# Up projection: eight products with high weight parts, then eight with low parts, where one of each took turns

## The chip, the core and the metric

The kernel runs on one core of a Trainium2 chip. The metric is device time in microseconds for one execution, as the median of several. Everything is float32 at the interface.

The engines that matter here are TensorE (matrix products; its weight loads are shown on a row of their own, PEld), VectorE (DVE), ScalarE (ACT), GpSimd (POOL) and SyncE (SP), which issues the transfers from memory.

## What is computed

One layer of a decoder trunk on 256 positions and 2048 channels. The sub-layer that the change touches, cut from the reference:

```python
h = rms_norm(x, norm2_g[l]) * (1.0 + scale2) + shift2
up = causal_dwconv(h @ w_up[l], ffn_dw_w[l], ffn_dw_b[l])    # w_up: 2048 x 11264
val, gt = jnp.split(up, 2, axis=-1)
x = x + gate2 * ((jax.nn.silu(gt) * val) @ w_down[l])        # w_down: 5632 x 2048
```

Before it stands a mixer sub-layer (an input projection, a causal convolution of width 31, a position mixing, an output projection), and shift, scale and gate come from a product of a conditioning vector with 2048 x 12288 weights.

## The kernel before

**Two-part operands.** TensorE multiplies operands in a reduced float32 form (float32r in the code). To keep float32 accuracy, an operand is split: `hi` is its rounded copy (ScalarE, line 154), `lo` is what is left (VectorE, line 155). A full product is then hi x hi + hi x lo + lo x hi.

**Weight tiles.** `load_split` brings in one tile of weights, 128 partitions x 2048 float32 (1 MB), into `raw` (4 buffers), and splits it into `hi` and `lo` (3 buffers each). It returns two halves of 1024 columns. Each half holds eight blocks of 128 x 128, for eight steps of the contraction.

**The up projection.** Its 11264 output columns are 88 blocks of 128: 44 value blocks and 44 gate blocks. The contraction over 2048 channels has `KT` = 16 steps of 128. The normalised activations are kept as a pair: `h2_of(k)` holds, for step k, 256 high values and behind them 256 low values per partition, 512 in one stretch. One product with the high part of the weights (`mm_up`, line 680) streams all 512 and writes 512 columns of an accumulator, which covers hi x hi and hi x lo. One product with the low part (line 681) streams the 256 high values alone and adds to the first 256 columns, which covers lo x hi. The accumulator is one bank of 128 x 512 float32. A block of weights is the operand that is loaded into the array; the activations are streamed.

`up_first` makes the first two column pairs, four accumulators at once, while the activations are still being made. `up(p)` makes each other pair of a value and a gate block, p = 2 to 43: for each of the two, one weight tile, 16 steps, and in each step a 512-wide product and a 256-wide one in turn. `up_f` then adds the two halves of the accumulators, applies the width-3 convolution, silu and the product, and splits the result for the down projection (lines 687 to 705, on ScalarE and VectorE).

**Order.** Each engine takes its instructions in program order, except where a few are given higher priority. `pump` puts pieces of background work (the modulation products of line 199, on VectorE with their own 1 MB transfers) behind each pair, by a credit in microseconds. The sequence is: `up_first`, `up` for pairs 2 to 23, the down projection of these (`down`, lines 183 to 185, products of 512 columns), `up` for pairs 24 to 43, the down projection of the rest.

Names in the profile: `pup` is the accumulator of the up projection, `hi_up`, `lo_up` and `raw_up` its weights, `h2a_h2b` its activations, `pod` the accumulator of the down projection, `pg`, `pu`, `pvc`, `pa`, `pco` those of stages in the mixer whose products are 256 wide, and `powo` that of the mixer's output projection (512 wide).

Of the kernel before, what the change touches and what calls it, by code (L numbers as in the profile page):

```python
# [17 lines left out]
P = 128  # L18
D = 2048
S = 256  # L20
NT = S // P
KT = D // P
# [44 lines left out]
def trunk(ctx, tc, xin, cvec, rows, wada, wa0, wa1, wv, wu, wg, wso, wco, wsT, wout, wup0, wup, wdn, out):  # L67
    nc = tc.nc
# [7 lines left out]
    def psum(name="ps"):  # L76
        return pp.tile([P, 512], F32, tag="ps", name=name)
# [86 lines left out]
    def load_split(src, name, places=None):  # L164

        raw = load_raw(src, name)
        if places is None:
            hi = wp.tile([P, 2048], F32R, tag="hi", name=f"hi_{name}", bufs=HI_BUFS)
            lo = wp.tile([P, 2048], F32R, tag="lo", name=f"lo_{name}", bufs=HI_BUFS)
        else:  # L170
            hi, lo = places[:, 0, :], places[:, 1, :]
        last["split"] = split(hi, lo, raw)
        return [(hi[:, h * 1024:(h + 1) * 1024], lo[:, h * 1024:(h + 1) * 1024]) for h in range(2)]
# [76 lines left out]
    def gate_half(j, kh):  # L250
        ps = psum(f"pg{kh}{j}")
        parts = load_split(wg[kh, j], f"g{kh}{j}")
        for half in range(2):
            hi, lo = parts[half]
            for kk in range(8):
                k = 8 * kh + kk
                cs = slice(kk * P, (kk + 1) * P)
                mm3(ps[:, half * S:(half + 1) * S], hi[:, cs], lo[:, cs], hH[:, k, :], hL[:, k, :], kk == 0, kk == 7)
        return ps

    for k in range(KT):
# [9 lines left out]
        hi = wp.tile([P, 2048], F32R, tag="hi", name=f"hi_a{k}", bufs=HI_BUFS)[:, :n0]  # L271
        lo = wp.tile([P, 2048], F32R, tag="lo", name=f"lo_a{k}", bufs=HI_BUFS)[:, :n0]
        split(hi, lo, raw)
        for j in range(4 + NV // 2):
            for half in range(2):
                cs = slice((2 * j + half) * P, (2 * j + half + 1) * P)
                mm3(pa[j][:, half * S:(half + 1) * S], hi[:, cs], lo[:, cs], hH[:, k, :], hL[:, k, :],
                    k == 0 and half == 0, k == KT - 1, skip_group_check=True)
        if k >= 8:
            for j in (2 * (k - 8), 2 * (k - 8) + 1):  # L280
                ps = gate_half(j, 0)
# [6 lines left out]
    def pump(phase, pe, dve):  # L288

        fill, share = SHARES[phase]  # L290
        us = fill * pe - dve
        if not (bg["conv"] and bg["ada"]):
            share = 1.0 if bg["conv"] else 0.0
        for key, part in (("conv", us * share), ("ada", us * (1 - share))):
            credit[key] += part
            while bg[key] and credit[key] >= bg[key][0][0]:
                cost, f = bg[key].pop(0)
                credit[key] -= cost
                f()
            if not bg[key]:  # L300
                credit[key] = 0.0
# [132 lines left out]
    for j in range(8):  # L434
        if j < NV:
            ps = pa[4 + j // 2][:, (j % 2) * S:(j % 2 + 1) * S]
        else:
            ps = psum(f"pvc{j}")[:, :S]
# [54 lines left out]
    for j in range(4, 8):  # L493
        ps = psum(f"pa{j}")
# [18 lines left out]
    for j in range(8):  # L513
        ps = psum(f"pu{j}")
# [7 lines left out]
    for j in range(KT):  # L522
        ps = gate_half(j, 1)
# [7 lines left out]
    for j2 in range(8):  # L531
        raw = load_raw(wso[j2], f"so{j2}")
        ps = psum(f"pso{j2}")
# [17 lines left out]
    for j2 in range(8):  # L551
        parts = load_split(wco[j2], f"co{j2}")
        ps = psum(f"pco{j2}")
# [104 lines left out]
    def h2_of(k):  # L658
        return h2[k // 8][:, k % 8, :, :]
# [14 lines left out]
    fslots = (2, 4, 5, 6, 0, 1)  # L674
    fH, fL = {}, {}

    def mm_up(ps, hi, lo, k):

        hk = h2_of(k)
        nc.tensor.matmul(ps, hi, hk.rearrange("p a s -> p (a s)"), start=(k == 0), stop=(k == KT - 1), skip_group_check=True)  # L680
        nc.tensor.matmul(ps[:, :S], lo, hk[:, 0, :], start=False, stop=(k == KT - 1), skip_group_check=True)  # L681

    def up_sum(dst, ps, jj):

# [8 lines left out]
    def up_f(p, ps):  # L693
        yv = t2(f"yv{p}").rearrange("p (h s) -> p h s", h=2)
        for half in range(2):
            up_sum(yv[:, half, :], ps[half], p + half * NF)
        sl = t1(f"sl{p}")
        nc.scalar.activation(sl, yv[:, 1, :], AF.Silu)
        f = t1(f"f{p}")
        nc.vector.tensor_tensor(f, yv[:, 0, :], sl, op=ALU.mult)  # L700
        if p % 4 == 0:
            ft = slot(fslots[(p // 4) % 6], [P, 4, 2, S], f"f{p}", F32R)
            for q in range(4):
                fH[p + q], fL[p + q] = ft[:, q, 0, :], ft[:, q, 1, :]
        split(fH[p], fL[p], f)

    def up(p):
        ps = [psum(f"pup{p}{half}") for half in range(2)]
        for half in range(2):
            parts = load_split(wup[2 * (p - 2) + half], f"up{p}{half}")  # L710
            for k in range(KT):
                hi, lo = parts[k // 8]
                cs = slice((k % 8) * P, (k % 8 + 1) * P)
                mm_up(ps[half], hi[:, cs], lo[:, cs], k)
        up_f(p, ps)
        pump("up", 10.3, 7.6)

    def up_first():

        ps = [psum(f"pup0{i}") for i in range(4)]  # L720
        for k4 in range(4):
            with ExitStack() as behind:
                if k4 >= 1:
                    behind.enter_context(tc.issue_after(last["dve"].ins))
                if k4 >= 2:
                    behind.enter_context(tc.issue_after(last["act"].ins))
                parts = load_split(wup0[k4], f"up0{k4}") if k4 else up0[0]
            for kk in range(4):
                k = 4 * k4 + kk
                i = make_h2(k)  # L730
                if k <= AFTER_K:
                    last["dve"] = i
                hi, lo = parts[kk // 2]
                for i in range(4):
                    cs = slice(((kk % 2) * 4 + i) * P, ((kk % 2) * 4 + i + 1) * P)
                    mm_up(ps[i], hi[:, cs], lo[:, cs], k)
        for p in range(2):
            up_f(p, ps[2 * p:2 * p + 2])
# [5 lines left out]
    for p in range(2, SEG):  # L744
        up(p)
# [4 lines left out]
    for p in range(SEG, NF):  # L750
        up(p)
# [79 lines left out]
```

## Time and profile before

| | |
|---|---|
| median of 3 runs | 1377.37 us (1373.61 to 1377.42) |
| profiled execution, its own time | 1376.01 us |
| its span, first to last instruction | 1374.3 us |
| mean granted TensorE clock | 0.986 |
| TensorE busy | 1327.7 us, 97% of the span |
| VectorE busy | 1073.5 us, 78% |
| ScalarE busy | 649.8 us, 47% |
| up projection, pairs 2 to 23 | about 654 to 899 us of the span |
| up projection, pairs 24 to 43 | about 1032 to 1255 us |

Times in the views count from the first instruction. A matmul's recorded duration runs from its start to its modelled end, and the next one starts before that end, so the distance between starts, not the duration, tells how fast TensorE takes them. In a row such as "128x512 f32", the number behind the x is how many columns a product streams.

### The profile page before, as it was taken

What the parts mean: (1) busy time and instruction counts of PE and PEld (TensorE: products, weight loads), DVE (VectorE), ACT (ScalarE), POOL (GpSimd) and SP (SyncE); (2) the same over time, 40 slices, a digit from 0 to 9 for tenths busy, and PEclk for the clock granted to TensorE, in tenths of its full rate; (3) what the DMA queues carried; (4) which work ended last, traced back from release to release, by engine and by line L of the source; (5) the groups of instructions that cost most, each with busy time, mean ns of one, the idle gap of its engine ahead of it and who ended that gap; (6) DMA issues with size and microseconds to landing.
All of it is one profiled execution on the core that took longest, in us unless ns stands there. A gap on an engine that the chain in (4) does not pass through costs nothing.

```text
span 1374.3 us, 19691 instructions
## 1 busy us (share of the span) xinstructions
PE 1327.7 (97%) x8170; PEld 1195.6 (87%) x8170; DVE 1073.5 (78%) x1319; ACT 649.8 (47%) x772; POOL 6.9 (1%) x18
## 2 busy tenths in 40 slices
PE   5689999999999999998999999999999999999997
PEld 4689999999999899887888888888888888888885
DVE  6987789999999698888998887754456776776573
ACT  5244464545551344445555555543334555555351
POOL 0000000000000000000000000000000000000000
PEclk9899999999999999998999999999999999999999
DMA  9999887687776898895877775555555555554551
GB/s 349 371 360 336 339 314 274 225 297 273 291 292 260 304 361 338 322 336 196 316 295 284 285 286 184 184 184 187 200 194 184 186 192 194 194 185 184 191 206 62
DMA packets 49481, 350.89 MB, mean 255 GB/s; under 512 B 5488, under 2 KB 5488, under 8 KB 8432
## 3 DMA queue, kind: packets, MB, share of 16 engines
q1 hardware_dynamic: 49392, 349.63, 68.6%
q8 instruction: 64, 1.05, 0.3%
q14 instruction: 25, 0.20, 0.0%
HBM read 347.51 MB, written 2.10 MB: 254 GB/s over the span
## 4 chain that ended last, share of the span: by engine, by line
PE 93%; DVE 3%; DMA 3%; ACT 1%; issue 0%; POOL 0%; ACTq 0%; POOLq 0%; SPq 0%
PE pup L680 24%; PE pup L681 12%; PE pod L184 6%; PE pod L183 6%; PE pod L185 6%; PE pg L179 4%; PE pg L177 4%; PE pg L178 4%; PE pso L537 4%; PE powo L184 2%; PE powo L185 2%; PE powo L183 2%; DVE ada L199 2%; PE pa L179 2%; PE pa L177 2%; PE pa L178 2%
## 5 line engine op out<-in xcount | busy, mean ns | idle before, releaser
L680 PE MATMUL pup<-h2a_h2b,hi_up 128*128 128x512 f32 x1408 | 494.1, 395 | 0.9 <-DVE h2a_h2b L237 0.9
L681 PE MATMUL pup<-h2a_h2b,lo_up 128*128 128x256 f32 x1408 | 395.7, 281 | 0.0
L680 PEld LDWEIGHTS pup<-h2a_h2b,hi_up 128*128 128x128 f32 x1408 | 266.3, 189 | 62.7 <-DVE h2a_h2b L237 1.3
L155 DVE TENSOR_TENSOR lo_up<-raw_up,hi_up 128x2048 fp32r<-128x2048 f32 x88 | 201.6, 2291 | 82.7 <-ACT hi_up L154 82.7
L681 PEld LDWEIGHTS pup<-h2a_h2b,lo_up 128*128 128x128 f32 x1408 | 265.0, 188 | 0.0
L199 DVE SCALAR_TENSOR_TENSOR ada<-ada,cbc 128x2048 f32<-128x2048 f32 x96 | 219.4, 2291 | 15.3 <-ACT cbc L129 7.7
L154 ACT ACTIVATE hi_up<-raw_up 128x2048 fp32r<-128x2048 f32 x88 | 168.6, 1916 | 110.0 <-PE pup L680 83.7
L155 DVE TENSOR_TENSOR lo_d<-raw_d,hi_d 128x2048 fp32r<-128x2048 f32 x42 | 96.3, 2292 | 92.2 <-ACT hi_d L154 92.2
L179 PE MATMUL pg<-hH_hL,lo_g 128*128 128x256 f32 x512 | 143.2, 280 | 0.4 <-DVE lo_g L155 0.4
L177 PE MATMUL pg<-hH_hL,hi_g 128*128 128x256 f32 x512 | 143.1, 279 | 0.0
L178 PE MATMUL pg<-hH_hL,hi_g 128*128 128x256 f32 x512 | 142.8, 279 | 0.0
L154 ACT ACTIVATE hi_d<-raw_d 128x2048 fp32r<-128x2048 f32 x42 | 80.5, 1916 | 107.1 <-PE pod L185 106.1
L184 PE MATMUL pod<-lo_d,f 128*128 128x512 f32 x332 | 129.2, 389 | 0.0
L183 PE MATMUL pod<-hi_d,f 128*128 128x512 f32 x332 | 129.2, 389 | 0.0
L185 PE MATMUL pod<-hi_d,f 128*128 128x512 f32 x332 | 129.2, 389 | 0.0
L179 PEld LDWEIGHTS pg<-hH_hL,lo_g 128*128 128x128 f32 x512 | 96.2, 188 | 0.6 <-DVE lo_g L155 0.6
L178 PEld LDWEIGHTS pg<-hH_hL,hi_g 128*128 128x128 f32 x512 | 96.0, 187 | 0.0
L177 PEld LDWEIGHTS pg<-hH_hL,hi_g 128*128 128x128 f32 x512 | 95.9, 187 | 0.0
L177 PE MATMUL pa<-hH_hL,hi_a 128*128 128x256 f32 x256 | 72.1, 300 | 19.6 <-ACT hH_hL L236 19.6
L155 DVE TENSOR_TENSOR lo_g<-raw_g,hi_g 128x2048 fp32r<-128x2048 f32 x32 | 74.5, 2328 | 18.5 <-ACT hi_g L154 18.5
L324 DVE SCALAR_TENSOR_TENSOR yc<-apad,cv,yc 128x256 f32<-128x256 f32 x200 | 85.7, 495 | 0.2
L689 ACT ACTIVATE yv<-pl,cv 128x256 f32<-128x256 f32 x88 | 50.9, 596 | 63.8 <-DVE pl L688 63.8
(196 smaller groups left out, 2299.5 us busy)
## 6 DMA issues: line engine op xcount, KB each, us to landing
ada<-in SPq DMA_DIRECT2D x96, 1024.0 KB, 5.8
raw_up<-in SPq DMA_DIRECT2D x88, 1024.0 KB, 4.8
raw_d<-in SPq DMA_DIRECT2D x44, 1024.0 KB, 4.8
raw_g<-in SPq DMA_DIRECT2D x32, 1024.0 KB, 6.2
raw_wo<-in SPq DMA_DIRECT2D x16, 1024.0 KB, 4.9
raw_a<-in SPq DMA_DIRECT2D x16, 640.0 KB, 5.6
raw_a<-in SPq DMA_DIRECT2D x8, 1024.0 KB, 4.8
raw_u<-in SPq DMA_DIRECT2D x8, 1024.0 KB, 4.9
```

What stands on the lines that cost most here:

```text
L154: nc.scalar.activation(hi, src, AF.Copy)
L155: return nc.vector.tensor_tensor(lo, src, hi.bitcast(F32), op=ALU.subtract)
L177: nc.tensor.matmul(ps, wH, aH, start=start, stop=False, **kw)
L178: nc.tensor.matmul(ps, wH, aL, start=False, stop=False, **kw)
L179: nc.tensor.matmul(ps, wL, aH, start=False, stop=stop, **kw)
L183: nc.tensor.matmul(ps, aH, wH, start=start, stop=False, **kw)
L184: nc.tensor.matmul(ps, aH, wL, start=False, stop=False, **kw)
L185: nc.tensor.matmul(ps, aL, wH, start=False, stop=stop, **kw)
L199: nc.vector.scalar_tensor_tensor(w, w, 1.0, cbc, op0=ALU.mult, op1=ALU.mult, accum_out=dst)
L324: nc.vector.scalar_tensor_tensor(ycf[:, j, :], src, cv[:, w0 + k:w0 + k + 1], ycf[:, j, :], op0=ALU.mult, op1=ALU.add)
L680: nc.tensor.matmul(ps, hi, hk.rearrange("p a s -> p (a s)"), start=(k == 0), stop=(k == KT - 1), skip_group_check=True)
L681: nc.tensor.matmul(ps[:, :S], lo, hk[:, 0, :], start=False, stop=(k == KT - 1), skip_group_check=True)
```

## The change

In `up`, the order of the 32 products of each weight tile is changed; `mm_up` is cut into two functions for it. Each half tile's eight products with the high part come first, for steps 0 to 7, then the eight with the low part, for the same steps. Then the second half follows likewise. The products themselves, their operands, the accumulators and the flags are the same. `up_first` keeps one of each in turn.

```diff
-    def mm_up(ps, hi, lo, k):
+    def mm_up_hi(ps, hi, k):
 
-        hk = h2_of(k)
-        nc.tensor.matmul(ps, hi, hk.rearrange("p a s -> p (a s)"), start=(k == 0), stop=(k == KT - 1), skip_group_check=True)
-        nc.tensor.matmul(ps[:, :S], lo, hk[:, 0, :], start=False, stop=(k == KT - 1), skip_group_check=True)
+        nc.tensor.matmul(ps, hi, h2_of(k).rearrange("p a s -> p (a s)"), start=(k == 0), stop=(k == KT - 1), skip_group_check=True)
+
+    def mm_up_lo(ps, lo, k):
+        nc.tensor.matmul(ps[:, :S], lo, h2_of(k)[:, 0, :], start=False, stop=(k == KT - 1), skip_group_check=True)
+
+    def mm_up(ps, hi, lo, k):
+        mm_up_hi(ps, hi, k)
+        mm_up_lo(ps, lo, k)
...
             parts = load_split(wup[2 * (p - 2) + half], f"up{p}{half}")
-            for k in range(KT):
-                hi, lo = parts[k // 8]
-                cs = slice((k % 8) * P, (k % 8 + 1) * P)
-                mm_up(ps[half], hi[:, cs], lo[:, cs], k)
+
+            for kh in range(2):
+                hi, lo = parts[kh]
+                for part, mm in ((hi, mm_up_hi), (lo, mm_up_lo)):
+                    for kk in range(8):
+                        mm(ps[half], part[:, kk * P:(kk + 1) * P], 8 * kh + kk)
```

## The prediction

> **What bounds the kernel now.** I read the page first: its span, the busy shares, the chain that ended last and the costliest groups. The chain's first line gives engines, its second names lines. In a group, the number before the bar is the count, then come busy time, mean ns of one, and idle time before the group with what ended it.
>
> ```profile
> span 1374.3 us, 19691 instructions
> ...
> PE 1327.7 (97%) x8170; PEld 1195.6 (87%) x8170; DVE 1073.5 (78%) x1319; ACT 649.8 (47%) x772; POOL 6.9 (1%) x18
> ...
> PE 93%; DVE 3%; DMA 3%; ACT 1%; issue 0%; POOL 0%; ACTq 0%; POOLq 0%; SPq 0%
> PE pup L680 24%; PE pup L681 12%; PE pod L184 6%; PE pod L183 6%; PE pod L185 6%; PE pg L179 4%; PE pg L177 4%; PE pg L178 4%; PE pso L537 4%; PE powo L184 2%; PE powo L185 2%; PE powo L183 2%; DVE ada L199 2%; PE pa L179 2%; PE pa L177 2%; PE pa L178 2%
> ...
> L680 PE MATMUL pup<-h2a_h2b,hi_up 128*128 128x512 f32 x1408 | 494.1, 395 | 0.9 <-DVE h2a_h2b L237 0.9
> L681 PE MATMUL pup<-h2a_h2b,lo_up 128*128 128x256 f32 x1408 | 395.7, 281 | 0.0
> ```
>
> TensorE is the bound: 93% of the chain, and 36% of it in the two lines that the change reorders. In all 2816 of their products it sat idle 0.9 us, once, at the very start. So there is no wait here to remove. Only the rate at which TensorE takes the products can change, and each ns per product goes straight to the end.
>
> The mean ns of a matmul overlaps its neighbours and is no rate. The rate comes from first and last start. The instructions by tile give these in a stretch (columns: count, duration min/median/max in ns, first to last start); for the accumulator of the up projection from 660 to 880 us:
>
> ```profile
> L680 PE MATMUL pup<-h2a_h2b,hi_up x632: 392/392/396, 659.8 to 879.9; 128*128 128x512 f32 x158
> L681 PE MATMUL pup<-h2a_h2b,lo_up x631: 278/280/283, 660.0 to 879.8; 128*128 128x256 f32 x158
> ```
>
> (879.9 - 659.8) us over 631 steps is 348.8 ns for a pair of one 512-wide and one 256-wide product. Half a weight tile is eight pairs, 2790 ns. The change makes that eight wide products and then eight narrow ones.
>
> **What runs of one width cost.** The same view for stages where one width repeats, the first two in threes (three lines take turns):
>
> ```profile
> L183 PE MATMUL pod<-hi_d,f x163: 389/389/389, 909.7 to 1019.9; 128*128 128x512 f32 x163
> ...
> L178 PE MATMUL pg<-hH_hL,hi_g x228: 279/279/279, 334.8 to 415.0; 128*128 128x256 f32 x114
> ...
> L177 PE MATMUL pco<-aH,hi_co x111: 283/283/283, 489.7 to 529.3; 128*128 128x256 f32 x111
> ```
>
> Wide in a run: 110.2 us / (162 x 3) = 226.7 ns. Narrow in a run: 80.2 us / (227 x 3) = 117.8 ns in the gates, 39.6 us / (110 x 3) = 120.0 ns in the conv output. The timeline (start, duration) holds a third steady rate for narrow ones, in a V tile:
>
> ```profile
> 206.17 0.28 PE L178 MATMUL pvc<-hH_hL,hi_v 128*128 128x256 f32 x1
> ...
> 211.27 0.28 PE L178 MATMUL pvc<-hH_hL,hi_v 128*128 128x256 f32 x1
> ```
>
> Fifteen rounds of three in 5.10 us is 113.3 ns, with moving data from the same pair of tiles as the gates. So the narrow rate has states, and I cannot tell from here which one a run of eight will fall into.
>
> 226.7 + 117.8 = 344.5 ns against 348.8 measured: taking turns costs 4.3 ns per pair more than the two widths cost in runs of their own. That is the whole prize. Pairs that the change touches: 42 column pairs x 2 halves = 84 weight tiles x 16 = 1344, in 168 half tiles (the other 64 of 1408, in the first two column pairs, keep their order).
>
> **The change, part by part.**
>
> *Wide run and narrow run.* 8 x (226.7 + 117.8) = 2756 ns against 2790: 34 ns less per half tile. Bounds for the narrow one: 113.3 and 120.0. For the wide one the lower end is 226.7; the upper comes from the border between up and down projection, where wide products start right behind a narrow one:
>
> ```profile
> 1255.32 0.28 PE L681 MATMUL pup<-h2a_h2b,lo_up 128*128 128x256 f32 x1
> 1255.44 0.39 PE L183 MATMUL pod<-hi_d,f 128*128 128x512 f32 x1
> 1255.67 0.39 PE L184 MATMUL pod<-lo_d,f 128*128 128x512 f32 x1
> ...
> 1257.28 0.39 PE L185 MATMUL pod<-hi_d,f 128*128 128x512 f32 x1
> ...
> 1031.92 0.39 PE L185 MATMUL pod<-hi_d,f 128*128 128x512 f32 x1
> 1032.14 0.40 PE L680 MATMUL pup<-h2a_h2b,hi_up 128*128 128x512 f32 x1
> 1032.38 0.28 PE L681 MATMUL pup<-h2a_h2b,lo_up 128*128 128x256 f32 x1
> ```
>
> The first eight steps there take 1.84 us, 230 ns each, before 226.7 is reached. I take the settled 226.7 and 117.8, since most rows of hundreds of products stand at them, and keep 230 and 120.0 as the dear end, 226.7 and 113.3 as the cheap one.
>
> *The switches.* Sixteen alternations become one switch each way. The first wide step after a narrow one was 0.23 us, about 3 ns over 226.7. The last wide step before a narrow one was 0.24 at 1032.14, but alternation was starting there; I take 3 ns for it too. Toll: 6 ns per half tile; between 0 and some 16 (13 at one by 1032.14, 3 at the other).
>
> *Waits for the split.* The first narrow product of a weight tile, which waits for VectorE's low part, moves back by seven wide products, 7 x 0.227 = 1.6 us. That gains nothing, as TensorE's waits in the whole program show (waiter, releaser: us, times, longest):
>
> ```profile
> PE pa L177 <- ACT hH_hL L236: 19.6, 9, 3.4
> ...
> PE pup L680 <- DVE h2a_h2b L237: 0.9, 1, 0.9
> ```
>
> No row names the up projection's weights. If VectorE fell behind, the new order would hide up to 1.6 us of it per tile; nothing is late, so I book zero.
>
> *Release of the high buffer.* The last wide product of a tile is now followed by eight narrow ones (8 x 0.118 = 0.94 us), where one followed (0.12 us). ScalarE's copy for the tile three on waits for just that release, and VectorE's subtraction for the copy:
>
> ```profile
> ACT hi_up L154 <- PE pup L680: 83.7, 54, 3.6
> ...
> DVE lo_up L155 <- ACT hi_up L154: 82.7, 64, 3.2
> ```
>
> Both, the release of the raw buffer and the next transfer in SyncE's queue behind it start up to 0.8 us earlier. Neither engine is late, so zero; what would be late next is VectorE, while the background modulation work runs:
>
> ```profile
> 654.00:700.00 46.00, 46.00 (x265) 40.28 (x265) 41.94 (x55) 25.98 (x36) 0.00 (x0) 1.00 0.82 310
> ```
>
> These are, for 654 to 700 us, length, busy time of TensorE, its loads, VectorE (41.94 of 46 us, 91%), ScalarE and GpSimd, the granted clock and DMA share. A tile shorter by 0.06 of 5.58 us asks 92% of VectorE: still covered. No instruction, byte or semaphore is added; start and stop flags fall on the same products.
>
> **The sum.** 34 - 6 = 28 ns x 168 = 4.7 us. The profiled execution took 1376.0 us, 1.7 over its span; it would take 1371.3, the span 1369.6. The median of the runs is 1377.37, so I forecast 1372.7 us. All of it must appear inside the two stretches of up projection.
>
> A rule that speaks against the change stands in the Trainium skill, "TensorE: Matmul & The Clock Gate", section Back-to-back issue gap: a warm product holds TensorE for its width at 2.4 GHz plus 2.5 ns. By it a pair is an estimated 215.8 + 109.2 = 325 ns in any order and the time would stay 1377.4. The trace has 226.7, 117.8 and 348.8 in those places, so a surplus that the rule lacks is there, and whether it follows order is the question; the section LDWEIGHTS of that page (128 columns, an estimated 107 ns) gives no preference either, since eight loads lie under narrow products in both orders.
>
> **The rivals.**
>
> *The settled rate is not reached* (24%). Eight wide products are just the unsettled stretch of 1255.44: 8 x (230 + 117.8) = 2782, 8 ns less, x 168 = 1.4 us: 1376.0. For: that border shows wide products straight behind a narrow one with no pause between, as each half tile now will, and they took seven steps to settle. Against: the down projection streams the weights and holds the activations, the other way round from here, so its settling need not carry over.
>
> *The surplus belongs to place, not order* (14%). The 4.3 ns could come from where the second normalised activations lie against the weights, for no other stage streams from them: no change, 1377.4. For: narrow rates of 117.8 and 120.0 differ with the stage. Against: 113.3 and 117.8 occur on the same tiles, so phase matters also without a move.
>
> *Cheap narrow state* (10%): 8 x (226.7 + 113.3) = 2720, 70 - 6 = 64 ns x 168 = 10.8 us: 1366.6.
>
> *Dear state* (4%): 8 x (230 + 120) = 2800, +10 ns x 168 = 1.6 us: 1379.0.
>
> *Slower: each switch restarts the load pipeline* (5%). Where a stage begins, the second product is late, as if its weights had not been fetched ahead:
>
> ```profile
> 285.47 0.36 PE L177 MATMUL pu<-hH_hL,hi_u 128*128 128x256 f32 x1
> 285.67 0.28 PE L178 MATMUL pu<-hH_hL,hi_u 128*128 128x256 f32 x1
> 285.79 0.28 PE L179 MATMUL pu<-hH_hL,lo_u 128*128 128x256 f32 x1
> ```
>
> 0.20 in place of 0.12. If both switches paid 0.085 us: 170 - 34 = 136 ns x 168 = 22.8 us, 1400.2. It makes the kernel slower by 0.3% from (34 + 25) / 2 = 30 ns per switch on. Against: width changed at every product so far without it, and at 1255.44 and 1032.14 the toll was 3 and 13 ns.
>
> **How the numbers follow.** The settled case holds the remaining 43%. Below, 0.3% (4.1 us) is about what a measurement can tell from no change. The settled case with a toll of 0 to 16 ns gives 5.7 to 3.0 us, so some three quarters of it, and the cheap state, count as faster: 0.32 + 0.10, and a little for a partly cheap narrow run in the unsettled case, 0.46. Slower: the restart and a share of the dear state, 0.07. The rest, 0.47, is the same. The range runs from the cheap state, 1366.5, to the dear one, 1379.0, and leaves out the restart and what lies beyond the bounds; the likeliest case alone spans 1371.7 to 1374.4.
>
> **What would show it.** Right: eight starts of the high line some 227 ns apart, then eight of the low line some 118 apart, 2.76 us per half tile, and the same stretches elsewhere to the ns. Starts of 230 throughout the high run show the second case; 113 in the low run the cheap one; a single step of 0.30 or 0.20 at a switch, the restart. The wait of ScalarE's copy for TensorE should shrink or move by about 0.8 us per tile without any end moving. The prediction is wrong if the wide rate on these activations has a floor above 227, if the narrow runs take 120, or if a wait for a low part appears on TensorE.

## The result, and the profile after

The changed kernel takes 1368.68 us (median of 8 runs, 1364.01 to 1370.60) against 1377.39 us for the kernel before (8 runs, 1372.58 to 1379.96). The ratio is 0.994, 95% interval 0.9925 to 0.9955: faster by 0.45 to 0.75%. A second comparison on another occasion, told below, gave 0.992, interval 0.9903 to 0.9938. The profiled execution took 1364.01 us, its span 1362.3.

From the page after: span, busy time by engine, the chain, and the groups of the up projection's products (now lines 679 and 682).

```profile
span 1362.3 us, 19690 instructions
...
PE 1318.1 (97%) x8170; PEld 1188.4 (87%) x8170; DVE 1072.2 (79%) x1319; ACT 649.3 (48%) x772; POOL 6.9 (1%) x18
...
PE 93%; DVE 4%; DMA 2%; ACT 1%; issue 0%; POOL 0%; ACTq 0%; POOLq 0%; SPq 0%
...
L679 PE MATMUL pup<-h2a_h2b,hi_up 128*128 128x512 f32 x1408 | 359.0, 392 | 0.9 <-DVE h2a_h2b L237 0.9
...
L682 PE MATMUL pup<-h2a_h2b,lo_up 128*128 128x256 f32 x1408 | 201.4, 279 | 0.0
```

TensorE is as much the bound as before and waits as little. The two groups' busy times are a trap: they add up to 560 us where they were 890, for a saving of some 6 us. Busy time is the union of overlapping spans, and turn-taking made the two lines overlap each other. The share of TensorE, 97% before and after, shows nothing of the change either. The Trainium skill warns that matmul busy time is no good measure of how close a kernel is to its roofline, the most that the engine could do ("Perfetto Trace Analysis", section Identifying the Most-Contended Engine). These traces agree: 97% in both, at two different rates.

What shows it is the distance between starts. The timeline after merges the runs of eight (start, time, line, count):

```profile
664.47 2.00 PE L679 MATMUL pup<-h2a_h2b,hi_up 128*128 128x512 f32 x8
666.30 1.07 PE L682 MATMUL pup<-h2a_h2b,lo_up 128*128 128x256 f32 x8
667.21 1.99 PE L679 MATMUL pup<-h2a_h2b,hi_up 128*128 128x512 f32 x8
669.03 1.11 PE L682 MATMUL pup<-h2a_h2b,lo_up 128*128 128x256 f32 x8
669.98 2.00 PE L679 MATMUL pup<-h2a_h2b,hi_up 128*128 128x512 f32 x8
```

Eight wide products take 1.83 and 1.82 us, 228 to 229 ns each; eight narrow ones take 0.91 us (113.8 each) in the first half of a tile and 0.95 (118 to 119) in the second. A tile is 669.98 - 664.47 = 5.51 us, where it was 16 x 348.8 ns = 5.58.

Where the profiled spans differ by 12.0 us, the first and last starts of the low-part products, and of the high-part ones, locate it. Before, then after:

```profile
L680 PE MATMUL pup<-h2a_h2b,hi_up x1408: 392/392/793, 628.9 to 1255.1; 128*128 128x512 f32 x176
...
L681 PE MATMUL pup<-h2a_h2b,lo_up x1408: 278/280/415, 629.5 to 1255.3; 128*128 128x256 f32 x176
```

```profile
L679 PE MATMUL pup<-h2a_h2b,hi_up x1408: 388/392/796, 623.8 to 1242.3; 128*128 128x512 f32 x176
...
L682 PE MATMUL pup<-h2a_h2b,lo_up x1408: 276/279/415, 624.4 to 1243.4; 128*128 128x256 f32 x176
```

The up projection began 5.1 us earlier; from its first to its last product it took 619.6 us in place of 626.4, 6.8 less; what follows took 119.0 and 118.9. Of the 6.8, about 5.8 are 84 tiles at 0.069 us. Some 1.2 lie in the first pairs, whose order did not change: up to the first read of an accumulator they took 24.5 us at a granted clock of 0.87 before, and 23.3 at 0.93 after (length, busy times, then the clock in the column after GpSimd's):

```profile
628.90:653.40 24.50, 24.45 (x124) 21.29 (x125) 21.86 (x33) 12.28 (x19) 0.00 (x0) 0.87 0.44 146
```

```profile
623.80:647.10 23.30, 23.29 (x124) 20.29 (x125) 22.04 (x33) 12.25 (x19) 0.00 (x0) 0.93 0.45 159
```

So the change accounts for 5.8 us between these two executions; the mixer's 5.1 and the first pairs' 1.2 needed an explanation, or to be shown as chance. For the first pairs, later profiles of the same two kernels gave 24.1 us at a clock of 0.90 and 23.7 at 0.91: their length went with the granted clock, and it moved by 0.4 us between executions of one kernel.

### The profile page after: what moved, and what is told of

Read it like the earlier page. It is cut to its first block, busy times and chain, and to the rows that moved or that the text cites. A ratio compares the mean times of both kernels' runs of the same rounds, so it can differ in the third digit from the quotient of the medians.

```text
span 1362.3 us, 19690 instructions
## 1 busy us (share of the span) xinstructions
PE 1318.1 (97%) x8170; PEld 1188.4 (87%) x8170; DVE 1072.2 (79%) x1319; ACT 649.3 (48%) x772; POOL 6.9 (1%) x18
## 4 chain that ended last, share of the span: by engine, by line
PE 93%; DVE 4%; DMA 2%; ACT 1%; issue 0%; POOL 0%; ACTq 0%; POOLq 0%; SPq 0%
PE pup L679 24%; PE pup L682 12%; PE pod L185 6%; PE pod L184 6%; PE pod L183 6%; PE pg L179 4%; PE pg L177 4%; PE pg L178 4%; PE pso L537 4%; PE powo L185 2%; PE powo L183 2%; PE powo L184 2%; DVE ada L199 2%; PE pa L179 2%; PE pa L177 2%; PE pa L178 2%
## 5 line engine op out<-in xcount | busy, mean ns | idle before, releaser
L679 PE MATMUL pup<-h2a_h2b,hi_up 128*128 128x512 f32 x1408 | 359.0, 392 | 0.9 <-DVE h2a_h2b L237 0.9
L679 PEld LDWEIGHTS pup<-h2a_h2b,hi_up 128*128 128x128 f32 x1408 | 253.0, 188 | 45.9 <-DVE h2a_h2b L237 1.3
L154 ACT ACTIVATE hi_up<-raw_up 128x2048 fp32r<-128x2048 f32 x88 | 168.6, 1916 | 96.5 <-PE pup L679 72.8
L682 PEld LDWEIGHTS pup<-h2a_h2b,lo_up 128*128 128x128 f32 x1408 | 192.4, 188 | 13.9
L682 PE MATMUL pup<-h2a_h2b,lo_up 128*128 128x256 f32 x1408 | 201.4, 279 | 0.0
L179 PEld LDWEIGHTS pg<-hH_hL,lo_g 128*128 128x128 f32 x512 | 96.2, 188 | 1.2 <-DVE lo_g L155 1.2
```

Source lines behind the costliest of these rows:

```text
L154: nc.scalar.activation(hi, src, AF.Copy)
L179: nc.tensor.matmul(ps, wL, aH, start=False, stop=stop, **kw)
L679: nc.tensor.matmul(ps, hi, h2_of(k).rearrange("p a s -> p (a s)"), start=(k == 0), stop=(k == KT - 1), skip_group_check=True)
L682: nc.tensor.matmul(ps[:, :S], lo, h2_of(k)[:, 0, :], start=False, stop=(k == KT - 1), skip_group_check=True)
```

## The experiments

A weight tile's time below is read from the instructions by tile, in a window that holds 40 whole tiles of the first stretch and the first product of the next: count 641, and (last - first start) / 40.

### The kernel before, once more

No edit.

> The kernel before once more, unchanged, for its spread. Theory A (only the rate at which TensorE takes the up projection's products changed): a weight tile of the up projection takes 5.58 us again, to the ns, while the start of the up projection (628.9 us before, 623.8 us after the change) moves by several us from one execution to another of the same kernel. Rival (the change also moves the mixer): the start stays within 1 us of 628.9.

It took 1378.02 us, span 1376.3. High-part products in the first stretch (40 tiles) and in the second (38 tiles):

```profile
L680 PE MATMUL pup<-h2a_h2b,hi_up x641: 392/397/398, 658.7 to 884.8; 128*128 128x512 f32 x161
...
L680 PE MATMUL pup<-h2a_h2b,hi_up x609: 392/392/396, 1039.7 to 1251.9; 128*128 128x512 f32 x153
...
L680 PE MATMUL pup<-h2a_h2b,hi_up x1408: 392/396/792, 628.1 to 1257.1; 128*128 128x512 f32 x176
```

226.1 us / 40 = 5.65 us a tile in the first stretch, 212.2 / 38 = 5.58 in the second. Theory A missed this: turn-taking has two rates, 353.3 and 348.8 ns a pair, and the same program falls into one or the other. The profile on which I predicted had the cheap one in both stretches. A dear first stretch costs 44 x 0.07 = 3.1 us more. In the timeline the dear pattern repeats after three pairs: 231, 117, 234, 123, 237, 118 ns between starts; the cheap one has 229 to 232 and 117 to 120. The start of the up projection, 628.1, lies within 1 us of 628.9, as the rival has it; that it moves without the change had yet to be seen.

### Runs of two and of sixteen

```diff
-            for kh in range(2):
-                hi, lo = parts[kh]
-                for part, mm in ((hi, mm_up_hi), (lo, mm_up_lo)):
-                    for kk in range(8):
+            for k0 in range(0, KT, 2):          # or 16
+                for which, mm in ((0, mm_up_hi), (1, mm_up_lo)):
+                    for k in range(k0, k0 + 2):
...
```

> Two products with high parts, then two with low parts, instead of eight and eight. Theory A1 (each switch of width costs something, about 34 ns saved per 8 pairs over 7 switches saved each way): half of the switches are gone, so about half of the gain, 5.55 us a weight tile. Theory A2 (no price per switch; the products fall into a repeating pattern whose phase the run length sets): anything between 5.49 and 5.60 us, not in proportion. Rival B (the earlier release of the high buffer brings the gain): the release comes 0.12 us earlier only, so 5.57 to 5.58 us.

> All sixteen products with high parts of a weight tile, then all sixteen with low parts. A1: half of the remaining switches gone, 5.508 us a tile or a little less than 5.513; if the wide ones settle at 226.7 ns after eight steps, 16 x 226.7 + 16 x 115 is about 5.48 us. A2: not in proportion, 5.49 to 5.60. B: released 0.94 us earlier again, so more of the gain, under 5.513 us.

1369.39 and 1369.62 us (one run each; the kernel before beside them 1378.21). In runs of two, then of sixteen:

```profile
L679 PE MATMUL pup<-h2a_h2b,hi_up x641: 388/392/394, 658.3 to 879.1; 128*128 128x512 f32 x161
```

```profile
L679 PE MATMUL pup<-h2a_h2b,hi_up x641: 388/392/397, 658.8 to 879.5; 128*128 128x512 f32 x161
```

5.520 us and 5.518, against 5.513 with eight. A price per switch (A1) falls: with four times the switches, runs of two lose 0.007 of the 0.069 us, where half was expected; halving the switches gains nothing. The release (B) does not fit either: runs of two release the buffer hardly earlier, and have nearly the whole gain. What costs is taking turns at every single product. That fits A2, a repeating pattern, though the spread that A2 allowed was wide.

### High parts last in the second half tile

```diff
-                for part, mm in ((hi, mm_up_hi), (lo, mm_up_lo)):
+                two = ((hi, mm_up_hi), (lo, mm_up_lo))
+                for part, mm in two if kh == 0 else two[::-1]:
```

> First half tile as in the changed kernel, second half with the low products first: runs of 8, 16 and 16, and the last high product ends the tile, so the high buffer is released later than even before the change. A: the rate of runs, 5.48 to 5.52 us a tile. B (release): no gain, 5.58 us or more, and a wait for the split on TensorE.

1369.93 us. The buffer's release is now the last thing that a tile does, and nothing is lost (its high-part products, then the row of TensorE's waits that names the up projection):

```profile
L679 PE MATMUL pup<-h2a_h2b,hi_up x641: 388/392/397, 658.8 to 879.5; 128*128 128x512 f32 x161
```

```profile
PE pup L679 <- DVE h2a_h2b L237: 1.3, 1, 1.3
```

220.7 / 40 = 5.518 us, and TensorE's only wait in the up projection is still the one at its start. The release (B) is no part of the gain.

### The accumulators apart

```diff
+        lows = [psum(f"plow{p}{half}")[:, :S] for half in range(2)]
...
-        nc.tensor.matmul(ps[:, :S], lo, hk[:, 0, :], start=False, ...)
+        nc.tensor.matmul(low, lo, hk[:, 0, :], start=(k == 0), ...)
...
         nc.vector.tensor_tensor(pl, pl, ps[:, :S], op=ALU.add)
+        nc.vector.tensor_tensor(pl, pl, low, op=ALU.add)
```

> The kernel before, one of each in turn, but in pairs 2 to 43 the low-part products add up in a bank of their own, so that consecutive products never write the same accumulator; VectorE adds the second bank with one more 256-wide instruction per block (some 0.42 us, 84 of them). Stream theory (the surplus of turn-taking lies in how streamed data and weight loads of changing length fall against each other): a weight tile takes 5.58 or 5.65 us as with one bank. Accumulator theory (it lies in two widths that write one bank in turn): the surplus goes, 5.51 us or less.

1376.97 us (the kernel before beside it 1375.80). The first three tiles, then 35 tiles from the ninth on, and four rows of the timeline between:

```profile
L680 PE MATMUL pup<-h2a_h2b,hi_up x49: 392/397/398, 654.3 to 671.3; 128*128 128x512 f32 x49
...
L680 PE MATMUL pup<-h2a_h2b,hi_up x561: 392/392/396, 699.6 to 895.0; 128*128 128x512 f32 x187
```

```profile
676.80 0.28 PE L684 MATMUL plow<-h2a_h2b,lo_up 128*128 128x256 f32 x1
677.07 0.70 PE L680 MATMUL pup<-h2a_h2b,hi_up 128*128 128x512 f32 x2
...
688.44 0.63 PE L680 MATMUL pup<-h2a_h2b,hi_up 128*128 128x512 f32 x2
688.91 0.40 PE L684 MATMUL plow<-h2a_h2b,lo_up 128*128 128x256 f32 x2
```

17.0 / 3 = 5.67 us and 195.4 / 35 = 5.58: the same two rates, so two widths in one bank are not the cause. The run also shows a change of pattern. It starts in the dear one. At 676.8 the steps are disturbed (0.27 us where 0.12 is usual, then two wide products in a row and two narrow ones), and by 678.5 the dear pattern is back. At 688.44 two wide and two narrow products come in a row again, this time without a pause, and behind them the cheap pattern stays for good. So the pattern hangs on how the sequence was entered.

### The streamed data moved

The pair of activations has some room in its buffer; `H_AT` places the mixer's pair, `H2_AT` the up projection's, in bytes.

```diff
-H_AT, H2_AT = 64, 320
+H_AT, H2_AT = 0, 0          # runs of eight; then 320, 64
+H_AT, H2_AT = 192, 0        # one of each in turn; then 448, 64
+H_AT, H2_AT = 192, 192      # runs of eight
```

> The changed kernel with the second pair of activations 320 bytes further down in its buffer (offset 0 in place of 320), as the conv output's activations lie; the first pair, which the mixer streams, at 0 in place of 64. Place theory (the surplus over the width hangs on where the streamed data lie against the weights): wide products settle at 226.7 ns and narrow ones at 120.0, as in the stages that lie so: 16 x 346.7 = 5.55 us a weight tile; the gates go from 117.8 to 120.0. Phase theory (the products fall into one of a few repeating patterns that order and start choose, wherever the data lie): 5.51 us a tile as before the move, the gates stay at 113.3 or 117.8.

> The changed kernel with the second pair at 64 in place of 320, where the mixer's pair lies, and the first pair at 320. Place theory: another rate than 5.513 us a tile, and the gates leave 117.8 for the rates seen in the up projection's narrow runs. Phase theory: 5.51 us, the gates at 113.3 or 117.8.

> The kernel before (one of each width in turn) with the second pair at 0 in place of 320, the first at 192. Place theory: the 348.8 and 353.3 ns a pair seen in two executions of the kernel before both go, to one new value, 346.7 by the stages that lie at 0. Phase theory: one of the two, 5.58 or 5.65 us a tile, or a third, not under 5.55, and it may change at the down projection between the two stretches.

> The kernel before with the second pair at 64, the first at 448. Place theory: a value of its own, different from that at 0. Phase theory: as at 0, 5.58 or 5.65 us a tile.

> The changed kernel with both pairs of activations at 192 in their buffer (64 and 320 before). With the first pair at 192 or 448 the gates ran at 113.3 ns a narrow product for long stretches. If the place decides which pattern the products fall into, the up projection's narrow runs all take 113.3 ns in place of 113.3 and 118 by halves: 5.513 - 8 x 0.0045 = 5.48 us a tile, and the gates start at 113.3. If the phase at the start of a stretch decides, 5.51 us, and the gates show either rate.

Single runs: 1382.80, 1368.05, 1376.43, 1372.55 (the kernel before beside these four 1374.95), and 1367.01 us (1375.80). In that order, high-part products of 40 tiles (behind the first a row of its gates, behind the fourth its second stretch):

```profile
L679 PE MATMUL pup<-h2a_h2b,hi_up x641: 389/393/398, 666.2 to 889.7; 128*128 128x512 f32 x161
...
L177 PE MATMUL pg<-hH_hL,hi_g x223: 283/283/283, 339.7 to 419.7; 128*128 128x256 f32 x112
```

```profile
L679 PE MATMUL pup<-h2a_h2b,hi_up x641: 388/392/394, 657.5 to 878.0; 128*128 128x512 f32 x161
```

```profile
L680 PE MATMUL pup<-h2a_h2b,hi_up x641: 395/398/403, 654.3 to 880.4; 128*128 128x512 f32 x161
```

```profile
L680 PE MATMUL pup<-h2a_h2b,hi_up x641: 392/397/398, 653.3 to 879.4; 128*128 128x512 f32 x161
...
L680 PE MATMUL pup<-h2a_h2b,hi_up x609: 392/392/396, 1034.3 to 1246.4; 128*128 128x512 f32 x153
```

```profile
L679 PE MATMUL pup<-h2a_h2b,hi_up x641: 388/393/398, 653.7 to 875.6; 128*128 128x512 f32 x161
```

| place of the up projection's pair | runs of eight | one of each in turn |
|---|---|---|
| 0 | 5.588 us | 5.653 in both stretches |
| 64 | 5.513 | 5.653, then 5.582 in the second stretch |
| 192 | 5.548 | not tried |
| 320 (as it was) | 5.513 | 5.582 or 5.653 |

Each pure theory was half right, and neither gave the tile times at 0 and 192 with runs (5.55 and 5.48 by place, 5.51 by phase). Place sets the rates: with runs of eight at 0, narrow products take 120.0 ns but the first, and every wide run starts with unsettled steps of 228 to 236, like those at the border in the prediction; the gates went from 117.8 to 80.0 us / (222 x 3) = 120.1 ns. But 64 and 320 give the same rates, and at either, turn-taking has the same two. Runs beat turn-taking at 0 too, by some 0.065 us a tile. That the run at 0 took 1382.80 us, more than the kernel before beside it, comes in good part from the mixer, whose pair was moved too: the 1536 products of the gates at 2.3 ns more are 3.5 us, and its up projection began only at 635.6 us. At 192 the narrow products take 113 to 114 ns, all but the first of each run (some 118), as expected by place, but the wide ones rise to 232.7, which I had not expected, so the tile is dearer.

### The changed kernel again, and with the mixer's pair moved

```diff
-H_AT, H2_AT = 64, 320
+H_AT, H2_AT = 192, 320
```

> The changed kernel itself, beside the next one and the kernel before on the same chip. The up projection's weight tile takes 5.513 us again in both stretches (one repeating pattern, not two): 5.8 us under an execution of the kernel before with 348.8 ns a pair throughout, 8.9 under one with 353.3 in the first stretch. Ratio to before 0.993 to 0.996.

> The changed kernel with the first pair of activations, which the mixer streams, at 192 in place of 64; the second stays at 320. If the place of the streamed data decides the gates' rate (113.3 ns at 192 in two executions; 117.8 in most and 113.3 in one at 64 or 320): 3 to 5 us under the changed kernel, ratio to before 0.990 to 0.993, the up projection at 5.513 us a tile. If the gates at 192 then wait for VectorE's low parts, less: 1 to 3 us. If the rate is chosen at random at the start, no difference.

The changed kernel: 1365.29 us (6 runs) against 1376.80 (11 runs), ratio 0.992, interval 0.9903 to 0.9938. With the move: 1363.50 us (5 runs), ratio 0.9899, interval 0.9883 to 0.9915. It is the fastest version that I ran, but 1.8 us under the changed kernel with overlapping intervals does not show that it is faster than that. The changed kernel, then the moved one with a row of its gates in the first 200 us and of the u stage:

```profile
L679 PE MATMUL pup<-h2a_h2b,hi_up x641: 388/392/394, 658.1 to 878.7; 128*128 128x512 f32 x161
...
L679 PE MATMUL pup<-h2a_h2b,hi_up x1408: 388/392/796, 628.1 to 1247.0; 128*128 128x512 f32 x176
```

```profile
L178 PE MATMUL pg<-hH_hL,hi_g x242: 280/281/282, 84.8 to 194.7; 128*128 128x256 f32 x121
...
L179 PE MATMUL pu<-hH_hL,lo_u x126: 275/276/277, 283.8 to 326.3; 128*128 128x256 f32 x126
```

The up projection's tile is 220.6 / 40 = 5.515 us again, and its start 628.1, where the first profile of the same kernel had 623.8. That is the chance asked for above: the 5.1 us in the mixer are no work of the change. Most of them can be named, and they are the same thing in another place. Seven tiles of gates in the first 200 us, in the first profile before, the first after and this one of the changed kernel:

```profile
L177 PE MATMUL pg<-hH_hL,hi_g x224: 279/279/279, 99.6 to 199.6; 128*128 128x256 f32 x112
```

```profile
L177 PE MATMUL pg<-hH_hL,hi_g x224: 276/276/277, 98.1 to 194.3; 128*128 128x256 f32 x112
```

```profile
L177 PE MATMUL pg<-hH_hL,hi_g x224: 279/279/279, 99.0 to 199.0; 128*128 128x256 f32 x112
```

They took 100.0 us, 96.2 and 100.0: in the first profile after, these gates ran in their cheap pattern, 3.8 us less, and in the second they did not.

In the moved kernel the durations tell the pattern: 276 ns goes with 113.3 ns between starts, 279 to 280 with 117.8, as in the rows of the prediction. The u stage has the cheap pattern (42.5 us / (125 x 3) = 113.3 ns), the gates in the first 200 us the dear one, although two executions with other kernels at 192 had the cheap one there. So 192 does not settle the gates' pattern. Nor does it take 192: the first profile after had the cheap pattern with the pair at 64.

## Why the prediction was right, and where not

**Direction, place and size.** Forecast 1372.7 us, 4.7 less; measured 1368.68, 8.7 less, inside the range and faster by more than 0.3%, but below the 1371.7 to 1374.4 of the likeliest case. The gain lies inside the two stretches and nowhere else that the change can be shown to reach.

**TensorE's rate, not a wait.** Right. No wait was removed (0.9 us idle before and after), and the run with the high parts last shows that the buffer's release is worth nothing. ScalarE's wait for it, forecast to shrink or move by up to 0.8 us a tile with no end moving, fell from 83.7 to 72.8 us over 54 times, 0.2 each:

```profile
ACT hi_up L154 <- PE pup L679: 72.8, 54, 2.7
```

**The terms of the sum.** The net was near, 34.5 ns a half tile (0.069 / 2 us) against 28, but by luck: the errors cancel. The wide run was put at a settled 226.7 ns; it takes 228.9 on average, and does not settle at 226.7 with the data at this place, not even in runs of sixteen. That is one of the signs that the prediction named for being wrong, a wide rate with a floor above 227, and in this term it was. The narrow run was put at 117.8; it takes that in one half tile and 113.3 in the other, so the cheap state, given 10% for all runs, holds for half of them. The toll for switches, 6 ns, cannot be told apart: runs of two, with four times as many, lose 3.5 ns a half tile in all.

**The step that was missed** is the baseline. I took 348.8 ns as what turn-taking costs, from one execution that had it in both stretches. The other profiled execution of the same kernel has 353.3 in the first, and against that the change gains 8.9 us, not 5.8. How common the dear pattern is can be read in part from the first two column pairs, which take turns in every version. Their high-part products before, then after the change (a median of 392 ns marks the cheap pattern, 397 the dear one, as in the rows of the kernel before once more):

```profile
L680 PE MATMUL pup<-h2a_h2b,hi_up x50: 392/392/396, 636.7 to 653.8; 128*128 128x512 f32 x50
```

```profile
L679 PE MATMUL pup<-h2a_h2b,hi_up x49: 392/397/398, 629.8 to 646.8; 128*128 128x512 f32 x49
```

Of the nine profiles with the pair at 320, three show the cheap pattern there (the first one, and the runs of two and of sixteen) and six the dear one, both profiles of the changed kernel among them. Where turn-taking went on behind the first pairs, the first stretch began in their pattern, in all five profiles. So the dear baseline is the usual one, as far as nine profiles tell, and the median gains of 8.7 and 11.5 us fit it better than 5.8. What is left over is within the mixer's own spread of some 5 us.

**The rivals.** "Surplus of place, not order" falls as it was put, since order changes the rate at 0, 64 and 320, but its mechanism is real: place sets what each order costs. "The settled rate is not reached" came true for the wide run in part (228.9 ns, against 230 there and 226.7 in the sum), while the narrow run came out cheaper than either had it. The dear state appeared only with the data moved to 0 (5.588 us a tile). The restart at each switch falls: no step of 0.30 or 0.20 us shows in the runs. The rule that a pair costs its widths in any order, worked out in the prediction from the Trainium skill ("TensorE: Matmul & The Clock Gate", section Back-to-back issue gap, which gives it for isolated products; an estimated 325 ns), has no place for what was measured: 344.6, 348.8 and 353.3 ns for the same two products.

**What is not settled** is the mechanism beneath. The runs show that the surplus depends on the order of the products, on the place of the streamed data and on how the sequence was entered, and not on the accumulator or on the number of switches as such. Why is open, and two things change together with the widths: in turns, the two products of a step stream the same activations one right behind the other, and the loads come from the high and the low buffer alternately; in runs, neither happens at every product. In the first two column pairs all eight products of a step stream the same activations, and the two rates are no higher there (17.1 us / 49 and 17.0 / 48 in the rows above), which speaks against the first of these. A version in which each narrow product follows one step behind would test it; none was run.

## What to carry to other kernels

When TensorE never waits, measure the distance between starts, not busy time, and compare it between stages: a few ns per product over thousands are the remaining gain, and the order of the products can hold them. Two products of the same width in a row were enough here. And take the baseline from more than one profiled execution, since one program can run at two rates.

## What the runs showed of the hardware

The same products in the same order fell into different repeating patterns, to the ns, for hundreds of microseconds: 348.8 or 353.3 ns a pair in turn-taking, 113.3 or 117.8 ns for narrow runs. A disturbance could change the pattern (two wide and two narrow products in a row at 688.44 us, with separate accumulators), and another one at 676.8 us did not. With the streamed data at 64 or 320 bytes in their buffer, wide products in runs of eight took 228.9 ns on average; at 192 they took 232.7. Narrow ones took 120.0 at 0, and 113.3 or 117.8 at the other places.
